# Memory's keys and values kept on chip: one pool of buffers in place of two, and stores issued by ScalarE

## The chip, the cores and the metric

The kernel runs on one core of one Trainium2 chip. The metric is the device time of one execution in microseconds (us). The engines are TensorE (PE; its weight loads are PEld), VectorE (DVE), ScalarE (ACT), GpSimd (POOL) and SyncE (SP), which here only issues transfers.

## The reference, cut to what matters

One layer of an encoder trunk over 1024 tokens of width 1024, in float32: latent attention and a Hyena operator side by side, then cross-attention into 256 memory tokens, then a mixture of experts. The change concerns only what the cross-attention takes from the memory tokens:

```python
def _mem_xattn(hx, hm, w_mq, w_mkv, w_mo):      # hm = _rms(mem, mem_norm_g): 256 x 1024
    q = (hx @ w_mq).reshape(B, S, MEM_HEADS, MEM_HEAD_DIM)        # 4 heads of 256
    k, v = jnp.split(hm @ w_mkv, 2, axis=-1)
    ...
    s = jnp.einsum('bshd,bmhd->bhsm', q, k).astype(jnp.float32) * MEM_HEAD_DIM ** -0.5
    p = jax.nn.softmax(s, axis=-1).astype(v.dtype)
    o = jnp.einsum('bhsm,bmhd->bshd', p, v).reshape(B, S, MEM_HEADS * MEM_HEAD_DIM)
    return o @ w_mo
```

Since `q k^T` is `hx (w_mq k^T)` and `(p v) w_mo` is `p (v w_mo)`, the kernel makes for each head the products of `w_mq` with the keys (KW) and of the values with `w_mo` (VW), both 1024 x 256 or 256 x 1024, once and ahead of time.

## The kernel before

**Split products.** Most matmuls work on pairs: `split` (line 196) rounds a float32 tile to a high part on ScalarE and subtracts it on VectorE for the low part; `mm3` (lines 204 to 208) adds three matmuls, high by high, high by low, low by high. A matmul of 256 or 512 columns in the profile is one of such three.

**Where memory's side stands.** `spectra` (line 287) is the first part of the program. It interleaves two streams of work that don't need each other: the filters of the Hyena operator (`filter_mlp`, `filters`: tiles `ph`, `win`, `eo`, `eoh`, `p`, `pp`, `q`, with tables `ftab` loaded by GpSimd's queue and results stored as `Kd` by SP's queue) and memory's side (`mem_side`, line 1198). Memory's side is a generator of 35 steps; `spectra` takes one or two of them after each step of the filters, until they are used up. When both are done, `x_rows` loads the tokens `xt` into the memory that they have left, and the projection follows. The order of tracing is the priority by which a planner fixes each engine's order of instructions at build time. On the chip each engine works through its own order, and a waiting instruction holds up those behind it.

**mem_side before.** First memory's rows are normalised and turned (`mx`, `mh` to `mmh`, `mml`). Then, in pools `mh` and `mhb`, 16 chunks of `w_mkv` (128 columns each, two for every head's keys, then two for every head's values): load `wm` (512 KB) by SP, split into `wmh`, `wml`, 24 matmuls of 256 columns into `pmk`, a copy by ScalarE to `mko`, and a store of 128 KB to `kvd` in HBM. Then these pools close and pool `mq` opens. For each of 4 heads of keys: `head` loads the head's two chunks back from `kvd` (`kv`, 256 KB) and splits them (`kvh`, `kvl`); `pair` splits two rows of `w_mq` (`qw` to `qwh`, `qwl`; `fetch` keeps two raw rows in flight); 48 matmuls make four `pkw` tiles; ScalarE scales them by `gc` into `mo` (line 1276, with high priority) and SP stores two 512 KB tiles of `mo` per head to KWd. For each of 4 heads of values the same with rows of `w_mo`: 24 matmuls of 512 columns (`pvw`), copies into `mo` (line 1292), two stores of 512 KB to VWd. KWd and VWd are read much later, by the cross-attention.

**PSUM.** The tiles `pmk`, `pkw` and `pvw` come from `psum1`, one bank each out of two buffers.

Of the kernel before, what the change touches and what calls it, by code (L numbers as in the profile page):

```python
# [9 lines left out]
F32 = mybir.dt.float32  # L10
F32R = mybir.dt.float32r
# [3 lines left out]
AF = mybir.ActivationFunctionType  # L15
ALU = mybir.AluOpType
# [6 lines left out]
P = 128  # L23
S = 1024
D = 1024
# [6 lines left out]
MEM = 256  # L32
MH, MHD = 4, 256
# [111 lines left out]
class Kern:  # L145
# [525 lines left out]
    def values(self):  # L671
        nc = self.nc
        self.ma = self.ma_cm.__enter__()
        self.V = self.ma.tile([P, NT, 512], F32, name="V")
        self.mla_rows(self.ma, self.key_rows(), 1)
        for i in range(NT):
            pv = self.psum1("pv")
            n, ts = i // 4, slice(i % 4 * P, i % 4 * P + P)
            (ch, cl), (wh, wl) = self.cqT[2], self.wm["v"]
            self.mm3(pv, ch[:, n, ts], cl[:, n, ts], wh, wl, True, True)  # L680
            nc.scalar.copy(self.V[:, i], pv)
            yield
# [515 lines left out]
    def mem_side(self):  # L1198

        nc, tc, a = self.nc, self.tc, self.a  # L1200
        kvd = self.dr.tile([16, P, MEM], F32, name="kvd")
        self.KWd = self.dr.tile([P, 8 * D], F32, name="KWd")
        self.VWd = self.dr.tile([P, 8 * D], F32, name="VWd")
        with tc.tile_pool(name="mh", bufs=1, side="right") as pa, tc.tile_pool(name="mhb", bufs=2, side="right") as pb:
            xts = [pb.tile([P, D], F32, tag="t4", name="mx", bufs=4) for i in range(2)]
            for i in range(2):
                nc.sync.dma_start(xts[i], a["mem"][i * P:(i + 1) * P])
            yield
            g = pb.tile([P, D], F32, tag="mw", name="mg")
            nc.sync.dma_start(g, a["mem_norm_g"].rearrange("(o n) -> o n", o=1).broadcast_to([P, D]))  # L1210
            mh = pa.tile([P, 8, MEM], F32R, name="mmh")
            ml = pa.tile([P, 8, MEM], F32R, name="mml")
            for i in range(2):
                h = self.rmsnorm(pb, xts[i], g, D, "m", 4)
                self.rows_T(pb, h, mh, ml, i)
                yield
            for c in range(16):
                w = pb.tile([P, 8, P], F32, tag="mw", name="wm")
                nc.sync.dma_start(w, a["w_mkv"][c])
                wh = pb.tile([P, 8, P], F32R, name="wmh")  # L1220
                wl = pb.tile([P, 8, P], F32R, name="wml")
                self.split(wh, wl, w)
                pk = self.psum1("pmk")[:, :MEM]
                for k in range(8):
                    self.mm3(pk, wh[:, k], wl[:, k], mh[:, k], ml[:, k], k == 0, k == 7)
                o = pb.tile([P, MEM], F32, name="mko")
                nc.scalar.copy(o, pk)
                nc.sync.dma_start(kvd[c], o)
                yield
        with tc.tile_pool(name="mq", bufs=2, side="right") as pb:  # L1230
            rows = [a["w_mqT"][j] for j in range(8)] + [a["w_mo"][j] for j in range(8)]
            raw = []

            def fetch():
                if rows:
                    w = pb.tile([P, D], F32, name="qw")
                    nc.sync.dma_start(w, rows.pop(0))
                    raw.append(w)

            fetch()  # L1240
            fetch()

            def pair():
                w = raw.pop(0)
                wh = pb.tile([P, D], F32R, name="qwh", bufs=3)
                wl = pb.tile([P, D], F32R, name="qwl", bufs=3)
                self.split(wh, wl, w)
                fetch()
                return wh, wl

            def head(j):
                t = pb.tile([P, 2, MEM], F32, name="kv", bufs=1)
                nc.sync.dma_start(t, kvd[j:j + 2].rearrange("c p m -> p c m"))
                th = pb.tile([P, 2, MEM], F32R, name="kvh")
                tl = pb.tile([P, 2, MEM], F32R, name="kvl")
                self.split(th, tl, t)
                return th, tl

            gc = pb.tile([P, 8], F32, name="gc", bufs=1)
            nc.sync.dma_start(gc, a["cross_norm_g"])  # L1260

            for h in range(MH):
                th, tl = head(2 * h)
                wp = [pair() for k in range(2)]
                for d0 in range(0, 8, 2):
                    pw = self.psum1("pkw")
                    if d0 % 4 == 0:
                        o = pb.tile([P, 4, MEM], F32, tag="mo", name="mo")
                    for d in range(2):
                        ds_ = slice((d0 + d) * P, (d0 + d + 1) * P)  # L1270
                        for k in range(2):
                            self.mm3(pw[:, d * MEM:(d + 1) * MEM], wp[k][0][:, ds_], wp[k][1][:, ds_], th[:, k], tl[:, k], k == 0, k == 1)
                    for d in range(2):
                        gd, src, j = gc[:, d0 + d:d0 + d + 1], pw[:, d * MEM:(d + 1) * MEM], d0 % 4 + d
                        with tc.high_priority():
                            nc.scalar.activation(o[:, j], src, AF.Identity, scale=gd)
                    if d0 % 4:
                        nc.sync.dma_start(self.KWd.rearrange("p (d m) -> p d m", d=8)[:, d0 - 2:d0 + 2, h * MEM:(h + 1) * MEM], o)
                        yield
            for h in range(MH):  # L1280
                th, tl = head(8 + 2 * h)
                wp = [pair() for k in range(2)]
                for mt in range(2):
                    ms = slice(mt * P, (mt + 1) * P)
                    o = pb.tile([P, 4, MEM], F32, tag="mo", name="mo")
                    for n in range(2):
                        pw = self.psum1("pvw")
                        ns = slice(n * 512, (n + 1) * 512)
                        for k in range(2):
                            self.mm3(pw, th[:, k, ms], tl[:, k, ms], wp[k][0][:, ns], wp[k][1][:, ns], k == 0, k == 1)  # L1290
                        with tc.high_priority():
                            nc.scalar.copy(o[:, 2 * n:2 * n + 2].rearrange("p a b -> p (a b)"), pw)
                    nc.sync.dma_start(self.VWd[:, (h * 2 + mt) * D:(h * 2 + mt + 1) * D], o.rearrange("p a b -> p (a b)"))
                    yield

    def cross_open(self):
        nc, tc, a = self.nc, self.tc, self.a
        self.h3d = self.dr.tile([S, D], F32, name="h3d")
        self.acc = self.dr.tile([S + NG * CAP, D], F32, name="acc")
        self.lg = self.late.tile([P, NT, 40], F32, name="lg")  # L1300
        self.route_init()
        wk = self.wk
        self.g3 = wk.tile([P, D], F32, tag="g", name="fg", bufs=1)
        nc.sync.dma_start(self.g3, a["ffn_norm_g"].rearrange("(o n) -> o n", o=1).broadcast_to([P, D]))
        self.wr = wk.tile([P, 8, 40], F32, name="wr")
        nc.sync.dma_start(self.wr, a["w_route"])
        gr = wk.tile([P, 8], F32, name="gr")
        nc.sync.dma_start(gr, a["ffn_gT"])
        nc.vector.tensor_tensor(self.wr, self.wr, gr[:, :, None].broadcast_to([P, 8, 40]), op=ALU.mult)
        self.br = self.bcast(wk, a["b_route"], 40, "br")  # L1310
        nc.vector.memset(self.br[:, 4:8], -3.0e38)
        self.hx, self.hT = {}, {}
# [790 lines left out]
```

## Time and profile before

| | before |
|---|---|
| time, median of 3 runs | 1499.66 us (1496.63 to 1503.1) |
| the profiled execution: its time / its span | 1501.6 / 1499.8 us |
| TensorE busy | 1373.0 us (92%), 6702 matmuls |
| VectorE / ScalarE / GpSimd busy | 1034.5 / 701.7 / 498.9 us |
| mean granted TensorE clock | 0.969 of full speed |

How to read the profile: it shows one execution, as seen by the hardware profiler. A row of the timeline has the start and duration in us, the engine (SPq is SP's queue of transfers), the line of the kernel, the operation, output <- inputs, shapes and count; in brackets, how long the engine idled before it and what ended that. A row of the lines view has a group's count, busy us and mean ns of one, then the idle time before it by what ended it. Matmuls overlap: the time from one start to the next is what one costs. The line of `mm3` (206 to 208) and `split` (196) are those of helpers, so tiles tell the stages apart.

### The profile page before, as it was taken

What the parts mean: (1) busy time and instruction counts of PE and PEld (TensorE: products, weight loads), DVE (VectorE), ACT (ScalarE), POOL (GpSimd) and SP (SyncE); (2) the same over time, 40 slices, a digit from 0 to 9 for tenths busy, and PEclk for the clock granted to TensorE, in tenths of its full rate; (3) what the DMA queues carried; (4) which work ended last, traced back from release to release, by engine and by line L of the source; (5) the groups of instructions that cost most, each with busy time, mean ns of one, the idle gap of its engine ahead of it and who ended that gap; (6) DMA issues with size and microseconds to landing.
All of it is one profiled execution on the core that took longest, in us unless ns stands there. A gap on an engine that the chain in (4) does not pass through costs nothing. (4 is left out here: it accounts for less than half of the span.)

```text
span 1499.8 us, 19038 instructions
## 1 busy us (share of the span) xinstructions
PE 1373.0 (92%) x6702; PEld 1025.5 (68%) x6702; DVE 1034.5 (69%) x1755; ACT 701.7 (47%) x1035; POOL 498.9 (33%) x363
## 2 busy tenths in 40 slices
PE   8888988999898989899899999999998999999990
PEld 5777767877787876565555788887886555666660
DVE  7655455389888888456657776434475598899985
ACT  6647446322212224434444344322232687888973
POOL 1321143354433242666666200000001238443322
PEclk9999999999999999999999999999999999999996
DMA  7458776343684525000311421004567899999995
GB/s 266 141 172 298 267 265 224 111 141 130 220 267 154 171 84 168 2 15 1 116 47 43 127 94 57 0 1 169 195 232 253 277 343 362 331 327 331 332 329 216
DMA packets 103406, 272.95 MB, mean 182 GB/s; under 512 B 13162, under 2 KB 41002, under 8 KB 103182
## 3 DMA queue, kind: packets, MB, share of 16 engines
q1 hardware_dynamic: 88590, 222.16, 42.3%
q0 software_dynamic: 14720, 49.57, 11.6%
q8 instruction: 53, 0.87, 0.2%
q14 instruction: 43, 0.35, 0.1%
HBM read 225.83 MB, written 50.07 MB: 184 GB/s over the span
## 5 line engine op out<-in xcount | busy, mean ns | idle before, releaser
L196 DVE TENSOR_TENSOR wt<-raw,wt 128x1024 fp32r<-128x1024 f32 x180 | 214.7, 1217 | 28.1 <-ACT wt L196 25.8
L196 ACT CAST wt<-raw 128x1024 fp32r<-128x1024 f32 x180 | 185.2, 1048 | 20.1 <-PE pgu L208 9.8
L994 POOL TENSOR_TENSOR sums<-sums,e 128x1024 f32<-128x1024 f32 x56 | 134.0, 2393 | 77.2 <-ACT e L990 75.4
L990 ACT ACTIVATE e<-psc 128x1024 f32<-128x1024 f32 x64 | 65.6, 1025 | 85.2 <-PE psc L208 81.9
L950 DVE TENSOR_REDUCE cn<-ptop 128x1 f32<-128x1024 f32 x64 | 75.7, 1211 | 41.2 <-PE ptop L949 40.8
L206 PE MATMUL pgu<-wt,xh 128*80 128x512 f32 x240 | 97.9, 408 | 0.0
L207 PE MATMUL pgu<-wt,xh 128*80 128x512 f32 x240 | 95.5, 398 | 0.0
L208 PE MATMUL pgu<-wt,xh 128*80 128x512 f32 x240 | 95.2, 397 | 0.0
L1835 POOL DMA_INDIRECT acc<-y,tab x28 | 51.2, 1827 | 118.9 <-ACT y L1832 100.7
L206 PE MATMUL psc<-xq,xk 97*128 97x512 f32 (+1 forms) x128 | 56.5, 441 | 11.3 <-ACT e L990 4.5
L1772 POOL DMA_INDIRECT xg<-h3d,tab x32 | 47.6, 1487 | 48.4 <-PE pxt L212 29.3
L999 PE MATMUL po<-e,V 128*64 128x512 f32 x256 | 58.5, 598 | 0.0
L362 POOL TENSOR_TENSOR eo<-win 128x512 f32<-128x512 f32 x16 | 23.8, 1488 | 87.8 <-DVE win L360 87.8
L206 PE MATMUL pw<-woh,ot 128*128 128x512 f32 x128 | 50.6, 395 | 1.6 <-DVE xr L1141 1.3
L207 PE MATMUL psc<-xq,xk 97*128 97x512 f32 (+1 forms) x128 | 52.0, 407 | 0.0
L208 PE MATMUL psc<-xq,xk 97*128 97x512 f32 (+1 forms) x128 | 52.0, 406 | 0.0
L233 POOL TENSOR_TENSOR fr<-fr0v,mhalf 128x1 f32<-128x1 f32 x4 | 2.3, 579 | 149.2 <-DVE fr0v L231 131.1
L572 ACT ACTIVATE uc<-pu,cw 128x1024 f32<-128x1024 f32 x12 | 14.5, 1209 | 78.6 <-PE pu L208 78.6
L206 PE MATMUL pcs<-kh,chh 128*128 128x512 f32 x128 | 50.4, 394 | 0.0
L207 PE MATMUL pw<-wol,ot 128*128 128x512 f32 x128 | 49.9, 390 | 0.0
L208 PE MATMUL pcs<-kh,chl 128*128 128x512 f32 x128 | 49.9, 389 | 0.0
L207 PE MATMUL pcs<-kl,chh 128*128 128x512 f32 x128 | 49.8, 389 | 0.0
(539 smaller groups left out, 4127.3 us busy)
## 6 DMA issues: line engine op xcount, KB each, us to landing
raw<-in_w_exp SPq DMA_DIRECT2D x192, 512.0 KB
tab<-in_t_cfwd POOLq DMA_DIRECT2D x32, 512.0 KB
ftab<-in_t_fwd POOLq DMA_DIRECT2D x16, 768.0 KB
wm<-in_w_mkv SPq DMA_DIRECT2D x16, 512.0 KB
Kd<-kts SPq DMA_DIRECT2D x16, 512.0 KB
kt<-Kd SPq DMA_DIRECT2D x32, 256.0 KB
tab<-in_t_inv SPq DMA_DIRECT2D x32, 256.0 KB
w<-in_w_hy SPq DMA_DIRECT2D x12, 512.0 KB
```

The source lines that it names most:

```text
L196: return self.nc.scalar.copy(hi, src).ins, self.nc.vector.tensor_tensor(lo, src, hi.bitcast(F32), op=ALU.subtract).ins
L206: mm(out, lh, rh, start=start, stop=False)
L207: mm(out, lh, rl, start=False, stop=False)
L208: mm(out, ll, rh, start=False, stop=stop)
L362: nc.gpsimd.tensor_tensor(t[:, 0], win[:, :512], win[:, 512:], op=ALU.add)
L572: nc.scalar.activation(y, pu, AF.Identity, scale=cw[:, c, 1:2], bias=cw[:, c, 3:4])
L950: nc.vector.tensor_reduce(cn[:, i, r:r + 1], ps, axis=AX.X, op=ALU.max, negate=True)
L990: nc.scalar.activation(e, ps, AF.Exp, scale=SCALE)
L994: nc.gpsimd.tensor_tensor(sums, sums, e, op=ALU.add)
L999: nc.tensor.matmul(po[par * 64:par * 64 + 64], V[:, kt, v], e[:, par * 512:(par + 1) * 512], start=kt == 0, stop=kt == NT - 1, skip_group_ ...
L1772: return nc.gpsimd.indirect_dma_start(out=x, out_offset=None, in_=self.h3d, in_offset=bass.IndirectOffsetOnAxis(ap=tok, axis=0), bounds_ch ...
L1835: scat = nc.gpsimd.indirect_dma_start(out=self.acc, out_offset=bass.IndirectOffsetOnAxis(ap=to, axis=0), in_=y, in_offset=None, bounds_che ...
```

## The change

`mem_side` keeps one pair of pools from beginning to end. Three kinds of 4 KB buffers (per partition), `mw` (raw, 2), `mwh` and `mwl` (3 each), hold memory's rows at first and then the raw, high and low weights of both kinds. The order of loads is a list: the two chunks of head 0, then for each of the 8 heads (4 of keys, 4 of values) its two chunks and the two rows of the head before. `values(h)` makes a head's two chunks and splits them straight from PSUM into `kvh`, `kvl`; `kvd` with its stores and loads is gone. The result of head h - 1 follows after the chunks of head h. Each `pkw` or `pvw` tile has its own `mo` buffer of 2 KB (two buffers, 4 KB before) and its own store of 256 KB, begun by ScalarE (`nc.scalar.dma_start`). `gc` is loaded at the beginning. The number of steps stays 35.

```diff
-            xts = [pb.tile([P, D], F32, tag="t4", name="mx", bufs=4) for i in range(2)]
+            W = lambda kind, name, dt=F32: pb.tile([P, D], dt, tag=kind, name=name, bufs=2 if kind == "mw" else 3)
+            xts = [W("mwh", "mx") for i in range(2)]
...
-            for c in range(16):
-                w = pb.tile([P, 8, P], F32, tag="mw", name="wm")
-                nc.sync.dma_start(w, a["w_mkv"][c])
-                wh = pb.tile([P, 8, P], F32R, name="wmh")
-                wl = pb.tile([P, 8, P], F32R, name="wml")
-                self.split(wh, wl, w)
-                pk = self.psum1("pmk")[:, :MEM]
-                for k in range(8):
-                    self.mm3(pk, wh[:, k], wl[:, k], mh[:, k], ml[:, k], k == 0, k == 7)
-                o = pb.tile([P, MEM], F32, name="mko")
-                nc.scalar.copy(o, pk)
-                nc.sync.dma_start(kvd[c], o)
-                yield
-        with tc.tile_pool(name="mq", bufs=2, side="right") as pb:
-            rows = [a["w_mqT"][j] for j in range(8)] + [a["w_mo"][j] for j in range(8)]
+            chunks = lambda h: [a["w_mkv"][2 * h + j].rearrange("p k c -> p (k c)") for j in range(2)]
+            rows = lambda h: [a["w_mqT" if h < MH else "w_mo"][2 * (h % MH) + j] for j in range(2)]
+            order = chunks(0)
+            for h in range(1, 2 * MH):
+                order += chunks(h) + rows(h - 1)
+            order += rows(2 * MH - 1)
             raw = []
...
             def pair():
                 w = raw.pop(0)
-                wh = pb.tile([P, D], F32R, name="qwh", bufs=3)
-                wl = pb.tile([P, D], F32R, name="qwl", bufs=3)
+                wh, wl = W("mwh", "mwhi", F32R), W("mwl", "mwlo", F32R)
                 self.split(wh, wl, w)
                 fetch()
                 return wh, wl
 
-            def head(j):
-                t = pb.tile([P, 2, MEM], F32, name="kv", bufs=1)
-                nc.sync.dma_start(t, kvd[j:j + 2].rearrange("c p m -> p c m"))
+            def values(h):
                 th = pb.tile([P, 2, MEM], F32R, name="kvh")
                 tl = pb.tile([P, 2, MEM], F32R, name="kvl")
-                self.split(th, tl, t)
-                return th, tl
+                for c in range(2):
+                    if len(raw) < 2:
+                        fetch()
+                    wh, wl = (t.rearrange("p (k c) -> p k c", k=8) for t in pair())
+                    pk = self.psum1("pmk")[:, :MEM]
+                    for k in range(8):
+                        self.mm3(pk, wh[:, k], wl[:, k], mh[:, k], ml[:, k], k == 0, k == 7)
+                    self.split(th[:, c], tl[:, c], pk)
+                    yield
+                kv[h] = th, tl
...
-                    if d0 % 4 == 0:
-                        o = pb.tile([P, 4, MEM], F32, tag="mo", name="mo")
+                    o = pb.tile([P, 2, MEM], F32, tag="mo", name="mo")
...
+                    nc.scalar.dma_start(self.KWd.rearrange("p (d m) -> p d m", d=8)[:, d0:d0 + 2, h * MEM:(h + 1) * MEM], o)
                     if d0 % 4:
-                        nc.sync.dma_start(self.KWd.rearrange("p (d m) -> p d m", d=8)[:, d0 - 2:d0 + 2, h * MEM:(h + 1) * MEM], o)
                         yield
...
                         with tc.high_priority():
-                            nc.scalar.copy(o[:, 2 * n:2 * n + 2].rearrange("p a b -> p (a b)"), pw)
-                    nc.sync.dma_start(self.VWd[:, (h * 2 + mt) * D:(h * 2 + mt + 1) * D], o.rearrange("p a b -> p (a b)"))
+                            nc.scalar.copy(o, pw)
+                        nc.scalar.dma_start(self.VWd[:, (h * 2 + mt) * D + n * 512:(h * 2 + mt) * D + (n + 1) * 512], o)
                     yield
+
+            kv = {}
+            mixed = lambda h: keys_mixed(h) if h < MH else values_mixed(h - MH)
+            yield from values(0)
+            for h in range(1, 2 * MH):
+                yield from values(h)
+                yield from mixed(h - 1)
+            yield from mixed(2 * MH - 1)
```

## Rows read from the trace of the kernel before

**Rows 1.** The page, part 1: busy us of each engine (share of the span).

```profile
PE 1373.0 (92%) x6702; PEld 1025.5 (68%) x6702; DVE 1034.5 (69%) x1755; ACT 701.7 (47%) x1035; POOL 498.9 (33%) x363
```

**Rows 2.** Stretches: length; PE, PEld, DVE, ACT, POOL busy; granted clock, DMA share, GB/s.

```profile
20.00:50.00 30.00, 27.95 (x195) 23.97 (x195) 25.33 (x35) 25.42 (x32) 0.00 (x0) 1.00 0.56 179
50.00:90.00 40.00, 36.04 (x239) 32.82 (x238) 22.91 (x18) 21.30 (x27) 16.82 (x11) 0.96 0.35 110
90.00:110.00 20.00, 14.86 (x78) 12.98 (x76) 12.99 (x9) 8.87 (x14) 6.10 (x6) 0.83 0.72 241
110.00:140.00 30.00, 24.73 (x172) 21.93 (x171) 19.23 (x19) 24.50 (x44) 6.20 (x5) 1.00 0.87 289
140.00:180.00 40.00, 38.42 (x165) 30.43 (x166) 18.28 (x17) 18.19 (x27) 4.96 (x6) 1.00 0.87 289
```

**Rows 3.** Timeline of TensorE, 92 to 108 us.

```profile
94.04 0.39 PE L208 MATMUL p<-eoh,ftab 128*128 128x512 f32 x1
94.27 0.39 PE L206 MATMUL p<-eoh,ftab 128*128 128x512 f32 x1
99.79 0.77 PE L206 MATMUL pkw<-kvh,qwh 128*128 128x256 f32 x2 [5.14 <-issue]
100.36 0.63 PE L207 MATMUL p<-eol,ftab 128*128 128x512 f32 x1
100.79 0.63 PE L208 MATMUL p<-eoh,ftab 128*128 128x512 f32 x1
...
106.27 0.28 PE L208 MATMUL pkw<-kvh,qwl 128*128 128x256 f32 x1
106.39 0.40 PE L206 MATMUL pp<-eoh,ftab 128*128 128x512 f32 x1
```

**Rows 4.** Timeline of the other engines, 86 to 100 us.

```profile
90.49 0.45 SPq L1253 DMA_DIRECT2D kv<-kvd  x1
...
95.09 1.04 ACT L196 CAST qwh<-qw 128x1024 fp32r<-128x1024 f32 x1 [6.51 <-DMA qw<-in_w_mqT]
...
99.08 0.62 ACT L196 CAST kvh<-kv 128x512 fp32r<-128x512 f32 x1 [1.50 <-DMA kv<-kvd]
```

**Rows 5.** Waits of SP's queue, 0 to 300 us: total, times, longest.

```profile
SPq L1228 <- ACT mko L1227: 38.9, 14, 6.6
...
SPq L470 <- PE ph L208: 16.7, 1, 16.7
```

**Rows 6.** Lines view of ScalarE, 20 to 180 us.

```profile
L196 ACT CAST qwh<-qw 128x1024 fp32r<-128x1024 f32 x16 | 16.9, 1054 | 11.7 <-DMA qw<-in_w_mqT 9.9 <-DMA qw<-in_w_mo 1.6
L196 ACT CAST wmh<-wm 128x1024 fp32r<-128x1024 f32 x15 | 15.6, 1048 | 5.9 <-DMA wm<-in_w_mkv 5.9
L1276 ACT ACTIVATE mo<-pkw,gc 128x256 f32<-128x256 f32 x32 | 13.4, 478 | 2.9 <-DMA KWd<-mo 1.9 <-PE pkw L208 1.0
...
L1292 ACT COPY mo<-pvw 128x512 f32<-128x512 f32 x16 | 9.1, 587 | 18.9 <-PE pvw L208 7.6 <-issue 5.7 <-DMA VWd<-mo 5.2
L1227 ACT COPY mko<-pmk 128x256 f32<-128x256 f32 x16 | 5.7, 364 | 4.8 <-PE pmk L208 3.8 <-issue 1.0
L196 ACT CAST kvh<-kv 128x512 fp32r<-128x512 f32 x8 | 5.0, 622 | 2.7 <-DMA kv<-kvd 2.7
```

**Rows 7.** Waits of TensorE, 20 to 180 us.

```profile
PE pmk L208 <- DVE wml L196: 5.2, 4, 3.1
...
PE pkw L206 <- ACT mo L1276: 2.5, 2, 1.7
```

**Rows 8.** Timelines of SP's queue and ScalarE around one store; the VWd stores (ns; first, last).

```profile
121.38 0.36 SPq L1278 DMA_DIRECT2D KWd<-mo  x1
...
127.60 0.84 ACT L1276 ACTIVATE mo<-pkw,gc 128x256 f32<-128x256 f32 x2 [1.90 <-DMA KWd<-mo]
...
L1293 SPq DMA_DIRECT2D VWd<-mo x8: 319/323/812, 144.2 to 180.3; - x8
```

More of the change, by code (lines that the diff above doesn't have):

```diff
@@ L1200, in mem_side @@
         nc, tc, a = self.nc, self.tc, self.a
-        kvd = self.dr.tile([16, P, MEM], F32, name="kvd")
         self.KWd = self.dr.tile([P, 8 * D], F32, name="KWd")
@@ L1208, in mem_side @@
             yield
-            g = pb.tile([P, D], F32, tag="mw", name="mg")
+            g = W("mw", "mg")
             nc.sync.dma_start(g, a["mem_norm_g"].rearrange("(o n) -> o n", o=1).broadcast_to([P, D]))
@@ L1212, in mem_side @@
             ml = pa.tile([P, 8, MEM], F32R, name="mml")
+            gc = pa.tile([P, 8], F32, name="gc")
+            nc.sync.dma_start(gc, a["cross_norm_g"])
             for i in range(2):
-                h = self.rmsnorm(pb, xts[i], g, D, "m", 4)
+                h, ss = W("mwl", "mh"), pa.tile([P, 1], F32, name=f"mss{i}")
+                nc.scalar.activation(h, xts[i], AF.Square, accum_out=ss)
+                r = self.rstd(pa, ss, D, f"mr{i}")
+                nc.vector.scalar_tensor_tensor(h, xts[i], r, g, op0=ALU.mult, op1=ALU.mult)
                 self.rows_T(pb, h, mh, ml, i)
                 yield
-            for c in range(16):
-                w = pb.tile([P, 8, P], F32, tag="mw", name="wm")
-                nc.sync.dma_start(w, a["w_mkv"][c])
-                wh = pb.tile([P, 8, P], F32R, name="wmh")
-                wl = pb.tile([P, 8, P], F32R, name="wml")
-                self.split(wh, wl, w)
-                pk = self.psum1("pmk")[:, :MEM]
-                for k in range(8):
-                    self.mm3(pk, wh[:, k], wl[:, k], mh[:, k], ml[:, k], k == 0, k == 7)
-                o = pb.tile([P, MEM], F32, name="mko")
-                nc.scalar.copy(o, pk)
-                nc.sync.dma_start(kvd[c], o)
-                yield
-        with tc.tile_pool(name="mq", bufs=2, side="right") as pb:
-            rows = [a["w_mqT"][j] for j in range(8)] + [a["w_mo"][j] for j in range(8)]
+            chunks = lambda h: [a["w_mkv"][2 * h + j].rearrange("p k c -> p (k c)") for j in range(2)]
[4 more added lines that the diff above has]
+            order += rows(2 * MH - 1)
             raw = []
             def fetch():
-                if rows:
-                    w = pb.tile([P, D], F32, name="qw")
-                    nc.sync.dma_start(w, rows.pop(0))
+                if order:
+                    w = W("mw", "mwr")
+                    nc.sync.dma_start(w, order.pop(0))
                     raw.append(w)
-            fetch()
             fetch()
@@ L1249, in pair, with keys_mixed @@
                 return wh, wl
-            def head(j):
-                t = pb.tile([P, 2, MEM], F32, name="kv", bufs=1)
-                nc.sync.dma_start(t, kvd[j:j + 2].rearrange("c p m -> p c m"))
+            def values(h):
                 th = pb.tile([P, 2, MEM], F32R, name="kvh")
                 tl = pb.tile([P, 2, MEM], F32R, name="kvl")
-                self.split(th, tl, t)
-                return th, tl
[L1259 to L1263, printed above, removed]
+                for c in range(2):
[8 more added lines that the diff above has]
+                kv[h] = th, tl
+            def keys_mixed(h):
+                th, tl = kv.pop(h)
                 wp = [pair() for k in range(2)]
@@ L1273, in mem_side, with values_mixed @@
                     for d in range(2):
-                        gd, src, j = gc[:, d0 + d:d0 + d + 1], pw[:, d * MEM:(d + 1) * MEM], d0 % 4 + d
+                        gd, src = gc[:, d0 + d:d0 + d + 1], pw[:, d * MEM:(d + 1) * MEM]
                         with tc.high_priority():
-                            nc.scalar.activation(o[:, j], src, AF.Identity, scale=gd)
+                            nc.scalar.activation(o[:, d], src, AF.Identity, scale=gd)
+                    nc.scalar.dma_start(self.KWd.rearrange("p (d m) -> p d m", d=8)[:, d0:d0 + 2, h * MEM:(h + 1) * MEM], o)
                     if d0 % 4:
-                        nc.sync.dma_start(self.KWd.rearrange("p (d m) -> p d m", d=8)[:, d0 - 2:d0 + 2, h * MEM:(h + 1) * MEM], o)
                         yield
-            for h in range(MH):
-                th, tl = head(8 + 2 * h)
+            def values_mixed(h):
+                th, tl = kv.pop(h + MH)
                 wp = [pair() for k in range(2)]
@@ L1284, in mem_side @@
                     ms = slice(mt * P, (mt + 1) * P)
-                    o = pb.tile([P, 4, MEM], F32, tag="mo", name="mo")
                     for n in range(2):
+                        o = pb.tile([P, 512], F32, tag="mo", name="mo")
                         pw = self.psum1("pvw")
```

## The prediction, made before the changed kernel was run

> **What bounds the kernel now.** The page's busy times come first [rows 1]. TensorE leads by far (92%); it works in order, so its holes are what can be won. Its busy time counts overlapped matmuls, so holes are looked for in stretches and in the timeline. The table of stretches [rows 2] covers the part in which memory's side (`mem_side`) runs beside the Hyena filters. It shows three things. 90 to 110 us is the worst stretch: TensorE busy 14.9 of 20 us at a mean granted clock of 0.83. ScalarE (ACT) is nearly full from 20 to 50 (25.4 of 30) and from 110 to 140 (24.5 of 30), and half idle between. The DMA engines stand at 0.87 from 110 to 180, at 0.35 from 50 to 90.
>
> The timeline of TensorE says what happens at 94 us [rows 3]. The `p` matmuls follow each other every 0.23 us; then the first `pkw` matmuls stand next in the queue, and nothing moves for 5.1 us. The work after it goes at half rate (0.43 us from start to start for 512 columns, the 1.2 GHz level after an idle engine) until about 105 us; at 106.2 the 256-column matmuls come every 0.12 us again. What the engine waited for is in the other timelines [rows 4]: the first keys are loaded back at 90.5, after the first pools have closed; ScalarE idles 6.5 us for the first rows of w_mq, loaded just before, then 1.5 us for the keys, whose cast begins at 99.1. It is the change of pools with the trip of the keys through memory that TensorE stands still for.
>
> A hole here moves everything behind it: the last gate of this part, the loads of x, waits on TensorE's own `ph` matmuls (the waits of SP's queue, 16.7 us) [rows 5], so all that follows begins earlier by what TensorE's order gains.
>
> **The change part by part.**
>
> *Pool change and kvd trip removed.* From the end of the last full-rate `p` (94.27 + 0.23 = 94.50) to the `pp` at 106.39 are 11.89 us. In them stand 5 `p` and 24 `pkw` matmuls: 5 x 0.23 + 24 x 0.12 = 4.0 us at full rate [rows 3]. So 7.9 us are lost, clock included. After the change keys_mixed(0) comes two chunks after its keys, in buffers that are already there: **-7.9 us**. From below: 5.1, if the clock drops elsewhere instead; from above 7.9.
>
> *Fewer and freer transfers.* 16 stores of 128 KB and 8 loads of 256 KB go (4 MB), and SP no longer holds loads behind stores: it waited 38.9 us in 14 places for `mko` before it could issue the next thing [rows 5]. What this can give is bounded by ScalarE's waits for transfers outside the hole [rows 6]: `wm` 5.9, `qw` 9.9 - 6.5 + 1.6 = 5.0, `kv` 2.7 - 1.5 = 1.2, and 5.2 for a VWd store, 17.3 in all. TensorE stood for splits of `wm` only 5.2 us [rows 7]. Between 0 and 5.2 I take **-2.5**: the loads themselves are as many and as big as before, with two raw buffers still, so about half of these waits should stay.
>
> The row says SP was not short of issue time, it waited. The Trainium skill (DMA: Bandwidth & Descriptors, section "Issuing engines are not separate DMA queues") goes further: a DMA begun on another engine runs on the same 16 engines, and only the sequencer's time for issuing is saved. By that rule the move of the stores alone is worth nothing and this term would be 0, the sum 1493.8; the trace agrees that the issue itself is short (0.36 us), but shows loads queued behind waiting stores, which the rule does not speak of.
>
> *ScalarE's work.* Gone: 16 `mko` copies x 0.364 = 5.8 us and 8 `kvh` casts x 0.622 = 5.0 us. New: 16 casts of 256 columns straight from PSUM, as `mko`'s row 0.364 = 5.8, and 32 store issues. No row has an issue on ScalarE; SP's takes 0.36 us [rows 8], so 32 x 0.36 = 11.5 us in which the activations behind it stand. Net +6.5 us in some 160 us. Activations (32 x 0.478) and copies (16 x 0.587) of the results stay [rows 6]. The first eight steps, which fall into 20 to 50 us, change most: eight chunks cost 8 x (1.048 + 0.364) = 11.3 us before; six chunks, two row splits, eight activations and four issues cost 8.5 + 2.1 + 3.8 + 1.4 = 15.8. With 25.4 of 30 us in use [rows 2] the added 4.5 us just fit, and from 110 us on ScalarE gets the lighter mix. Bounds 0 and +6.5; I take **+1.5**, a third of the 4.5, since in-order engines don't fill gaps fully. If that cover is gone, it is 4.5. VectorE subtracts the same elements as before, from PSUM, in 16 pieces for 8; its added fixed costs lie in its idle time (18.3 of 40 us busy at 140 to 180). But the PSUM buffer of a chunk is now freed by VectorE's subtraction, not by ScalarE's copy alone; with two such buffers shared by chunks and results, the second `pkw` of a head waits for it. Bounded by a `kvh` wait and by nothing, it is in the 1.5.
>
> *Half-size result buffers.* `mo` keeps two buffers, each now half as big, and a store per buffer. ScalarE's next activation into a buffer waits for its store to land, and every cast queued behind it on ScalarE waits too. The one store that can be timed was issued at 121.38 and let the activation go at 127.60: 6.2 us for 512 KB at a DMA share near 0.87 [rows 2, 8]. A store of 256 KB takes between half of that (3.1) and all of it. The side's 32 steps end with the last VWd store at 180.3 [rows 8]; taken from 17 us on, when memory's rows are turned, they are 5.1 us each, and the later ones make two results each: one per 2.5 us, so a buffer is wanted again 2 x 2.5 - 0.95 (two activations) = 4.1 us after it was filled. Each of the two later results of a head (16 in all) waits 0 to 2.1 us: 0 to 34 us of ScalarE. Of its waits for `mo` stores before (1.9 + 5.2 [rows 6]) TensorE saw up to half (2.5 for ACT `mo` [rows 7]), so 0 to +17. I take **+0.5**: the DMA engines carry 4 MB less and more evenly, which is nearer to 3.1 than to 6.2.
>
> TensorE's own work does not change (384 + 192 + 96 matmuls, the same shapes), nor does the number of steps that `spectra` takes from the side (35), nor the work per step: 24 matmuls of 256 columns (2.9 us) or 12 of 512 (2.8 us). Raw loads stay at two buffers. Nothing after 240 us is touched.
>
> Sum: -7.9 - 2.5 + 1.5 + 0.5 = **-8.4 us**. The profiled execution took 1501.6 (span 1499.8), 1.9 above the median 1499.66: it would come to 1493.2, and the median to **1491.3 us**. What this measurement can tell from no change is about 0.5%, 7.5 us (the three runs span 6.5), so the forecast lies just past it.
>
> **The rivals.**
>
> *More is won (0.20).* The evened load of ScalarE and of the DMA engines takes most of the other waits too: all 5.2 us for `wm` splits, and the 2.5 for ACT `mo` [rows 7]. For it: both loads are lopsided now [rows 2]. Against it: the waits for splits come from in-order queues as much as from late loads. -7.9 - 5.2 - 2.5 = -15.6, **1484**.
>
> *The hole goes, the gain is eaten (0.22).* Work that ScalarE gets between 20 and 50 us fully shows (+4.5), the loads' waits all stay, and in each of 8 heads the second result waits one cast of 0.364 for its PSUM buffer (+2.9): the hole is only spread. -7.9 + 7.4 = -0.5, **1499**. For it: ScalarE has 4.6 us left in that stretch. This is also the case in which the change doesn't do what it says, the weights' three shared buffers making chunk and result wait for each other.
>
> *Slower (0.18).* The two half buffers of `mo` wait for each store: at 6.2 us a store, 16 waits of 2.1 us, half of them seen by TensorE, are +17: -8.4 - 0.5 + 17 = +8.1, **1507.8**. It decides from a landing time of about 5.2 us on, where 16 waits of 1.1, half of them seen, are 8.8 us and eat the gain. For it: the one timed store. Against it: 256 KB, less traffic. The Trainium skill (Perfetto Trace Analysis, section "DMA Optimizations") speaks for this one: batching small transfers into larger ones raises throughput, and it names 2 KB to 4 KB; here VWd's rows go from 4 KB to 2 KB and the stores double in number. The trace before has no 2 KB store to set beside it.
>
> **How the numbers follow.** The forecast has 0.40, around 1491.3 (1487 to 1496), of which some 0.6 lie below 1492.2, the mark for faster by over 0.5%. Faster: 0.24 + 0.20, and a little of the third case, 0.46. Slower: 0.18. Same: 0.36. The range leaves out one tenth at each end: down into the second case, 1481, up to the last, 1507.
>
> **What would show it.** Right: no wait of 5 us before the first `pkw`; the granted clock at its full level there; the x loads 6 to 10 us earlier; matmul counts as before; ScalarE busier from 20 to 50. The second term: shorter waits for `wm`. The third: `pkw` or chunk matmuls waiting for casts before 50 us. The fourth: ScalarE's waits for KWd or VWd stores under about 3 us in all. Wrong: many such waits of 1 to 2 us, or TensorE's holes as long in sum as before but scattered; or a gain that is lost after 240 us, where I assume a plain shift.

## The result, and the profile after

The changed kernel takes 1512.88 us (median of 6 runs; one of them, 1937.32 us at a granted clock of 0.649, is left out of the ratio) against 1502.32 us for the kernel before on the same chip: ratio 1.0063, 95% interval 1.0040 to 1.0085. It is slower by 0.6%; faster by 0.6% was forecast. The profiled execution took 1512.82 us, its span is 1511.0.

Busy time of the engines (part 1 of the page, as [rows 1]) hardly moves:

```profile
PE 1378.7 (91%) x6702; PEld 1029.8 (68%) x6702; DVE 1032.0 (68%) x1763; ACT 695.2 (46%) x1025; POOL 500.2 (33%) x363
```

Same table of stretches as [rows 2], after:

```profile
20.00:50.00 30.00, 24.47 (x152) 19.84 (x151) 25.73 (x39) 20.65 (x29) 0.00 (x0) 0.89 0.57 176
50.00:90.00 40.00, 35.47 (x227) 30.35 (x226) 27.19 (x26) 28.09 (x39) 18.76 (x12) 1.00 0.46 150
90.00:110.00 20.00, 18.59 (x131) 16.43 (x129) 9.33 (x9) 11.49 (x18) 2.81 (x4) 1.00 0.78 240
110.00:140.00 30.00, 23.91 (x136) 21.76 (x136) 14.29 (x14) 14.49 (x22) 3.03 (x3) 0.89 0.58 197
140.00:180.00 40.00, 35.89 (x170) 29.60 (x168) 20.75 (x20) 15.40 (x21) 9.04 (x7) 0.96 0.65 222
```

The hole at 94 us is gone: 131 matmuls at full clock stand between 90 and 110, where there were 78 at 0.83. But 20 to 50 and 110 to 180, at full clock before, now run at 0.89 to 0.96 with a less busy TensorE. The first `pu` matmul, which follows this part, begins at 256.4 us; before it was 245.9. So the loss of about 10 us is made before it, and what follows (1254.6 us to the end of the span, 1253.9 before) is a plain shift.

What TensorE waits for, 20 to 200 us, after (against [rows 7]; `mwr`, `mwhi` and `mwlo` are the raw, high and low weights of both kinds):

```profile
PE pmk L206 <- ACT mo L1274: 6.2, 4, 3.6
PE pkw L208 <- DVE mwlo L196: 4.3, 3, 1.8
PE pvw L206 <- ACT mo L1291: 2.6, 1, 2.6
PE pmk L206 <- ACT mo L1291: 2.5, 1, 2.5
PE pkw L206 <- DVE kvl L196: 2.0, 1, 2.0
```

Waits for the eviction of a result (ACT `mo`) come to 11.3 us; before they were 2.5 for `pkw` and 1.2 for `pvw`. ScalarE's own waits in the same stretch say what holds these evictions up (against the `mo` rows of [rows 6]):

```profile
ACT mo L1291 <- DMA VWd<-mo: 12.2, 5, 4.9
ACT mo L1274 <- DMA KWd<-mo: 7.5, 2, 4.9
```

19.7 us for stores still under way, against 7.1 before. One of these waits in ScalarE's timeline, then in TensorE's the last matmul of the third result and the matmul that the wait holds back:

```profile
105.62 0.84 ACT L1274 ACTIVATE mo<-pkw,gc 128x256 f32<-128x256 f32 x2 [0.59 <-PE pkw L208]
106.49 0.37 ACTq L1275 DMA_DIRECT2D KWd<-mo  x1
106.96 0.84 ACT L1274 ACTIVATE mo<-pkw,gc 128x256 f32<-128x256 f32 x2 [0.50 <-ACT mo L1274]
107.83 0.37 ACTq L1275 DMA_DIRECT2D KWd<-mo  x1
112.74 0.84 ACT L1274 ACTIVATE mo<-pkw,gc 128x256 f32<-128x256 f32 x2 [4.94 <-DMA KWd<-mo]
```

```profile
107.92 0.28 PE L208 MATMUL pkw<-kvh,mwlo 128*128 128x256 f32 x1
...
113.63 0.39 PE L206 MATMUL pmk<-mmh,mwhi 128*128 128x256 f32 x1 [3.56 <-ACT mo L1274]
```

Two results are evicted 1.3 us apart and fill both buffers. The third is ready at 108.2, 1.7 us after the store of the first was begun (106.49), and waits for it until 112.74: that store took 6.25 us. Until then its PSUM bank is not free, and the next chunk (`pmk`) needs that bank. The view of the tile `mo` gives the issue of a store on ScalarE and the time to landing, in ns and us (min, median, max):

```profile
L1275 ACTq DMA_DIRECT2D KWd<-mo x16: 366/366/396, 42.5 to 115.3; - x16
L1292 ACTq DMA_DIRECT2D VWd<-mo x16: 326/326/343, 124.3 to 185.4; - x16
...
DMA to landing us min/median/max: 2.0/3.1/7.8
```

The waits of SP's queue, 20 to 240 us (against [rows 5]), are no longer for `mko`. Its loads now wait for the raw buffers that VectorE's subtractions free (91.9 us; before, `qwl` and `wml` together, 40.0), and the x loads behind them for TensorE's `ph`, as before:

```profile
SPq L1234 <- DVE mwlo L196: 91.9, 22, 9.1
SPq L407 <- DVE kts L406: 40.7, 9, 17.4
SPq L470 <- PE ph L208: 18.0, 1, 18.0
```

### The profile page after: what moved, and what is told of

It is laid out like the page before. It is cut to its first block, busy times and chain, and to the rows that moved or that the text cites. A ratio compares the mean times of both kernels' runs of the same rounds, so it can differ in the third digit from the quotient of the medians.

```text
span 1511.0 us, 18993 instructions
## 1 busy us (share of the span) xinstructions
PE 1378.7 (91%) x6702; PEld 1029.8 (68%) x6702; DVE 1032.0 (68%) x1763; ACT 695.2 (46%) x1025; POOL 500.2 (33%) x363
## 5 line engine op out<-in xcount | busy, mean ns | idle before, releaser
L196 DVE TENSOR_TENSOR mwlo<-mwr,mwhi 128x1024 fp32r<-128x1024 f32 x32 | 40.0, 1254 | 26.9 <-ACT mwhi L196 26.8
```

Source lines behind the costliest of these rows:

```text
L196: return self.nc.scalar.copy(hi, src).ins, self.nc.vector.tensor_tensor(lo, src, hi.bitcast(F32), op=ALU.subtract).ins
```

## The experiments

Each ratio is to the kernel before, measured on the same chip in the same session, with its 95% interval. "First pu" is where that matmul begins in the one profiled execution of a kernel; these executions lie up to 12 us from the median of their kernel, so small differences in it prove little.

**Result buffers (E1 to E6).** Theory: the two half-size `mo` buffers wait for their stores. Rivals: who begins the stores, or the weights' shared buffers and the order of the work.

E1, four half-size buffers in the changed kernel (shown for `pkw`, the same for `pvw`). Room for them comes from opening the pool of two small attention tiles later:

```
-                    o = pb.tile([P, 2, MEM], F32, tag="mo", name="mo")
+                    o = pb.tile([P, 2, MEM], F32, tag="mo", name="mo", bufs=4)
```

> The changed kernel with four result buffers (mo) of 2 KB in place of two; the 4 KB for it come from opening the pool of kr and cn (3 KB) after the filters instead of before. Theory A (the two half-size result buffers wait for their stores; ScalarE stands, and the PSUM bank behind it holds TensorE): ScalarE's waits for KWd and VWd stores fall from 19.7 us to under 3, TensorE's waits for mo (11.3 us) to under 3, and the time falls by 9 to 14 us against the changed kernel, to a ratio of 0.995 to 1.001 against the kernel before. Theory B (bursts of weight splits in the three shared buffers, and keys split out of PSUM by two engines, set the holes): the waits for stores go too, but others take their place, ratio 1.004 to 1.007.

1.0027 (1.0003 to 1.0052), first pu 250.1; ScalarE waits 2.2 us for stores, TensorE 1.7 for evictions. The waits go as theory A said, but the time falls by 5 us against the changed kernel and not by 9 to 14: it lies between the two forecasts. TensorE's waits for weight splits rise from 6.7 to 12.3 us.

E2, the result tiles of before (two of 4 KB, 16 stores of 512 KB) in the changed kernel, still begun by ScalarE:

```
-                    o = pb.tile([P, 2, MEM], F32, tag="mo", name="mo")
+                    if d0 % 4 == 0:
+                        o = pb.tile([P, 4, MEM], F32, tag="mo", name="mo")
...
-                        nc.scalar.dma_start(self.VWd[:, (h * 2 + mt) * D + n * 512:(h * 2 + mt) * D + (n + 1) * 512], o)
+                    nc.scalar.dma_start(self.VWd[:, (h * 2 + mt) * D:(h * 2 + mt + 1) * D], o.rearrange("p a b -> p (a b)"))
```

> The changed kernel with the result tiles and stores of the kernel before (two buffers of 4 KB, 16 stores of 512 KB), still begun by ScalarE, same 3 KB of room. Theory A, if the room in buffers is what counts: as with four buffers of 2 KB, ratio 0.995 to 1.002. If it is the number of stores in flight that counts, two stores of 512 KB still wait: ScalarE's waits for stores 4 to 10 us, ratio 1.000 to 1.005. Theory B: 1.004 to 1.007.

1.0005 (0.9987 to 1.0024); first pu 245.4. ScalarE's waits for stores and TensorE's for evictions:

```profile
ACT mo L1297 <- DMA VWd<-mo: 3.9, 1, 3.9
```

```profile
PE pvw L206 <- ACT mo L1297: 3.2, 1, 3.2
PE pmk L206 <- ACT mo L1280: 1.9, 1, 1.9
```

E3, the changed kernel with its 32 stores begun by SP (`nc.sync.dma_start` for `nc.scalar.dma_start`):

> The changed kernel with its 32 stores begun by SP instead of ScalarE, nothing else. Theory A: SP's queue also holds the loads, which wait for raw buffers (92.6 us in 23 places), so a store goes out later, the result buffers come free later, and the time grows by 5 to 20 us over the changed kernel, ratio 1.010 to 1.020. Theory C (the issue on ScalarE is the cost: 32 x 0.35 = 11 us of ScalarE): the time falls by 4 to 10 us, ratio 0.999 to 1.004.

1.0106 (1.0087 to 1.0126), first pu 260.8. In SP's queue the stores wait for the evictions, and the loads stand behind them; ScalarE's waits for weights to arrive rise from 7.6 to 19.4 us:

```profile
SPq L1275 <- ACT mo L1274: 32.6, 16, 4.6
SPq L1292 <- ACT mo L1291: 28.0, 12, 6.4
```

E4, the kernel before with nothing but the half-size result buffers, stored in 256 KB pieces begun by ScalarE:

> The kernel before with one part of the change alone: each pkw or pvw tile has its own 2 KB result buffer (two of them), stored by ScalarE as 256 KB. Theory A: slower by 5 to 15 us, ratio 1.003 to 1.010, with 10 us or more of ScalarE waiting for KWd and VWd stores. Theory B: no change beyond 3 us, ratio 0.998 to 1.002.

1.0093 (1.0071 to 1.0116), first pu 265.7. Its ScalarE waits 19.0 us for stores, its TensorE 14.2 for evictions, with the hole still there (`issue`):

```profile
ACT mo L1275 <- DMA KWd<-mo: 10.9, 6, 3.1
ACT mo L1291 <- DMA VWd<-mo: 4.1, 4, 1.5
ACT mo L1291 <- DMA KWd<-mo: 4.0, 1, 4.0
```

```profile
PE pvw L206 <- ACT mo L1291: 8.3, 4, 3.1
PE pkw L206 <- issue: 5.9, 1, 5.9
PE pkw L206 <- ACT mo L1275: 5.2, 7, 1.5
```

E5, control: the changed kernel with the later pool alone (`kr` and `cn` from a pool opened after the spectra):

> The changed kernel with only the two small tiles of the attention part (kr, cn) moved into a pool that opens later, which is how the four-buffer and the big-buffer kernels found their room; result buffers stay two of 2 KB. If the result buffers alone explain what those kernels won back, this one stands where the changed kernel does: 1.004 to 1.009 of the kernel before, ScalarE waiting 15 to 20 us for KWd and VWd stores before 200 us. If the later pool itself helped, it comes to 1.000 to 1.003, and the credit given to the buffers was wrong.

1.0054 (1.0029 to 1.0078), 18.1 us of waits for stores: the pool explains nothing.

E6, the kernel before with its 512 KB stores begun by ScalarE:

> The kernel before with its 16 result stores of 512 KB begun by ScalarE in place of SP, nothing else. If the loss of the half-size result buffers alone (1.0093) comes from their size, this one stays within 0.3% of the kernel before, with 4 to 8 us of ScalarE's waits for stores as before. If it comes from ScalarE issuing the stores, it goes to about half of that loss or more (half as many issues of 0.35 us): 1.004 to 1.009.

0.9971 (0.9953 to 0.9990): not a loss but a gain of 4 us, the lowest ratio of all kernels here that leave nothing out. ScalarE's waits for stores (7.5 us before) are gone, and TensorE's for evictions fall from 3.7 to 0.8; ScalarE's waits for loads do not fall (20.1 before, 22.9). So it is the result buffers that come free sooner, and not the loads that arrive sooner. Its first pu (247.6) is no earlier in the profile, so where the 4 us are won is not shown.

Half-size buffers in the kernel before thus cost 1.0093 (E4) against 0.9971, some 18 us, and as much by the first pu (265.7 against 247.6). In the changed kernel they cost 1.0063 against 1.0005 (E2), some 9 us (256.4 against 245.4 by the first pu). The theory holds for the size of the buffers; four half-size ones (E1) win back about 5 us only.

**Where the hole's gain went (E7 to E17).** E2 has no hole and few waits for stores (3.9 us), and yet only equals the kernel before. TensorE's waits between 20 and 200 us add up to 17.7 us in it; before, they are 18.5, of which 5.1 are the hole. The stretch in which the first results are made shows a part of this. Two windows of it, columns as in [rows 2]; first the kernel before, then the changed kernel, then E2:

```profile
28.00:36.00 8.00, 7.15 (x58) 6.74 (x57) 7.63 (x13) 7.94 (x11) 0.00 (x0) 1.00 0.52 182
36.00:44.00 8.00, 6.80 (x46) 5.44 (x46) 7.71 (x10) 7.16 (x9) 0.00 (x0) 1.00 0.47 146
```

```profile
28.00:36.00 8.00, 5.53 (x36) 4.12 (x34) 5.83 (x10) 5.61 (x9) 0.00 (x0) 1.00 0.49 147
36.00:44.00 8.00, 6.04 (x23) 4.17 (x22) 6.47 (x12) 5.42 (x10) 0.00 (x0) 0.57 0.28 81
```

```profile
28.00:36.00 8.00, 6.24 (x40) 4.68 (x39) 7.28 (x13) 6.43 (x10) 0.00 (x0) 1.00 0.45 143
36.00:44.00 8.00, 6.66 (x37) 5.50 (x36) 7.11 (x11) 5.99 (x11) 0.00 (x0) 0.79 0.39 132
```

In the changed kernel TensorE waits there for two of VectorE's results:

```profile
35.53 0.39 PE L206 MATMUL pkw<-kvh,mwhi 128*128 128x256 f32 x1 [1.99 <-DVE kvl L196]
39.11 0.58 PE L208 MATMUL pkw<-kvh,mwlo 128*128 128x256 f32 x1 [1.82 <-DVE mwlo L196]
```

But VectorE is less busy in these 16 us than before (12.30 us for 15.33). It stands for a cast of ScalarE, which stands for its load:

```profile
29.84 1.05 ACT L196 CAST mwhi<-mwr 128x1024 fp32r<-128x1024 f32 x1 [1.49 <-DMA mwr<-in_w_mqT]
30.92 1.23 DVE L196 TENSOR_TENSOR mwlo<-mwr,mwhi 128x1024 fp32r<-128x1024 f32 x1 [1.79 <-ACT mwhi L196]
```

And a load waits for a raw buffer, which VectorE's subtraction frees, so that each of the three waits for another.

E7, E2 with weights split up to two tiles ahead of their use:

```
+            def ahead(n):
+                while len(made) < n and raw:
...
                     self.split(th[:, c], tl[:, c], pk)
+                    ahead(2)
                     yield
```

> The changed kernel with the big result buffers (two of 4 KB, 512 KB stores) and the weights split up to two tiles ahead of their use: the rows of w_mq and w_mo are split in the steps of the chunks before them, the next chunk during the results. Same buffers, same loads in the same order. If the gain of the removed hole was eaten by splits that begin only when their result step does (waits of TensorE for mwlo and mwhi, 8 to 10 us between 15 and 200 us), these waits fall to under 4 us and the time to 0.995 to 0.998 of the kernel before. If these waits only show another limit (ScalarE and VectorE in order, the two raw buffers, loads), the waits move to other tiles and the time stays at 0.999 to 1.002, as with the big buffers alone.

0.9985 (0.9957 to 1.0012), first pu 247.0: not to be told from E2. TensorE still waits 6.8 us for weight splits (8.5 in E2) and 2.9 for `kvl` (1.6). E8, besides, the chunks' splits at the planner's high priority:

> As the kernel with weights split ahead, and besides the split of a chunk's keys or values out of PSUM (kvh, kvl) is given the planner's high priority, as the result evictions have. In the changed kernel the first pkw stands 2.0 us for kvl at 33 us. If that wait is from VectorE's order, it goes, and the time falls by up to 2 us against the kernel without it (0.995 to 0.997 of before). If the planner then puts other work later, there is no difference or a small loss.

1.0006 (0.9982 to 1.0030): no gain; TensorE still waited 1.7 us for `kvl` at 33.7 us. E9, E7 with GpSimd in VectorE's place for four weight tiles:

```
+                    if k in (4, 5, 8, 9):
+                        nc.scalar.copy(wh, w)
+                        nc.gpsimd.tensor_tensor(wl, w, wh.bitcast(F32), op=ALU.subtract)
```

> The kernel with big result buffers and weights split ahead, in which GpSimd (idle from 20 to 50 us) makes the low halves of the w_mq rows of the first two heads, four subtractions of 128x1024, in VectorE's place. In all kernels with keys on chip TensorE stands 3 to 4 us at the first pkw (33 to 40 us) for kvl and mwlo, both VectorE's, and then goes at half clock from 36 to 44 us; the kernel before does neither. If VectorE's queue in that stretch is what eats the gain of the removed hole, the mwlo waits there go, the clock stays up, and the time falls by 3 to 6 us against the kernel without it (to 0.994 to 0.997 of before). If the first result step is late for another reason (loads, ScalarE, the longer chain of casts), the low clock from 36 to 44 us stays and so does the time (0.998 to 1.001).

1.0039 (1.0014 to 1.0065): worse than either forecast, though its first pu (246.4) is no later than E7's; the clock is 0.50 from 36 to 44. The timelines of GpSimd and VectorE show why this did not relieve VectorE:

```profile
30.87 2.37 POOL L1254 TENSOR_TENSOR mwlo<-mwr,mwhi 128x1024 fp32r<-128x1024 f32 x1 [20.00 <-ACT mwhi L1253]
38.63 2.84 POOL L1254 TENSOR_TENSOR mwlo<-mwr,mwhi 128x1024 fp32r<-128x1024 f32 x1 [5.39 <-ACT mwhi L1253]
```

```profile
29.78 0.68 DVE L279 SCALAR_TENSOR_TENSOR u<-k,u 64x512 f32<-64x512 f32 x1
31.43 2.35 DVE L279 SCALAR_TENSOR_TENSOR u<-k,u 64x512 f32<-64x512 f32 x1
37.85 4.17 DVE L279 SCALAR_TENSOR_TENSOR u<-k,u 64x512 f32<-64x512 f32 x3
```

E10, the first result one head later (`bufs=3` for `kvh` and `kvl`, half-size result buffers), and E11, its control with two:

> The changed kernel with weights split ahead (half-size result buffers), and three buffers for a head's keys or values in place of two, so that six chunks stand ahead of the first result and the first pkw comes two chunks later, after the filter's first stage. If the first result step collides with the filter's start on VectorE, the waits at 33 to 40 us and the low clock after them go or get shorter, and the time is 3 to 6 us under the control with two buffers. If the waits only move with it, it equals the control within 2 us.

> Control for the later first result: the changed kernel with weights split ahead and the later pool for two small tiles, half-size result buffers. If waiting for stores is what the changed kernel loses by, splitting ahead does not help it: 1.003 to 1.007 of before, ScalarE still waiting 15 to 20 us for stores. If the splits were the cause, it is at 0.998 to 1.001.

E10: 1.0085 (1.0053 to 1.0116); E11: 1.0064 (1.0036 to 1.0092), with 14.3 us of waits for stores. Later is no better. The wait moved with the result (3.3 us for `kvl` at 45 us). E12, E6 with four low halves of chunks on GpSimd:

> The kernel before with its 512 KB stores begun by ScalarE, and the low halves of chunks 3 to 6 of w_mkv made by GpSimd in VectorE's place. TensorE waited 2.8 us for these (wml) between 29 and 43 us. If VectorE's queue is what TensorE waits for there, these waits go and the time falls by 2 to 3 us more (0.994 to 0.997 of before); if GpSimd's subtraction, slower than VectorE's 1.2 us, comes later than VectorE's would, the time is the same or 1 to 3 us longer.

1.0046 (1.0020 to 1.0072): 11 us worse than E6, more than forecast; TensorE waits for GpSimd instead, up to 2.0 us a tile. E13, shared buffers and no change of pools, but all chunks first and keys through memory:

```
+            order = sum([chunks(h) for h in range(2 * MH)], []) + sum([rows(h) for h in range(2 * MH)], [])
...
+                tl = kv.pop(h)
+                th = pb.tile([P, 2, MEM], F32R, name="kvh")
+                self.split(th, tl, tl.bitcast(F32))
+                load(h + 1)
```

> Half of the change: weights of both kinds share buffers and are split ahead, results are stored in 512 KB pieces begun by ScalarE, but all 16 chunks come first and keys and values still go through memory (eight 256 KB stores, eight loads one head ahead). So there is no change of pools and no hole at the first pkw, and no early results between the chunks. If the hole was worth its 7.9 us, and it is the early results among the chunks that cost it again, this kernel beats the kernel before with stores by ScalarE (0.9971): 0.991 to 0.994 of before. If removing the hole is worth little wherever it is done, because TensorE then stands for something else, it is at 0.996 to 0.999.

1.0013 (0.9987 to 1.0038), first pu 248.0: neither theory. The hole at 94 us is gone here too, but another of the same size opened at 68 us, where the chunk's weight cast stands behind an `eoh` cast that waits for GpSimd:

```profile
73.50 0.58 PE L206 MATMUL pmk<-mmh,mwhi 128*128 128x256 f32 x1 [5.54 <-ACT mwhi L196]
```

```profile
71.18 1.05 ACT L196 CAST eoh<-eo 128x1024 fp32r<-128x1024 f32 x1 [4.81 <-POOL eo L363]
72.40 1.99 ACT L196 CAST mwhi<-mwr 128x1024 fp32r<-128x1024 f32 x2
```

E14, E7 without VectorE's early low halves (`wl = wh` for 14 weight tiles, `tl = th` for three heads), and E15, the same for ten chunks of E6:

> The kernel with big buffers and weights split ahead, with part of the work left out: for the first 14 weight tiles and the first three heads' keys the low half is not made (VectorE's subtraction), and TensorE uses the high half in its place, with the same matmuls. It stands against the same omission in the kernel before (next run). If VectorE's subtractions are why the first 50 us got worse with the keys on chip, the waits at 33 to 40 us and the half clock after them go, and this one gains 4 to 6 us against the kernel with them (to 0.994 to 0.996), more than the kernel before gains by it. If ScalarE's casts or the loads are what is late there, it gains 2 us or less.

> The kernel before with 512 KB stores by ScalarE, with part of the work left out: for the first ten chunks the low half of the weights is not made, and TensorE uses the high half in its place. TensorE waited 2.8 us for these subtractions before 50 us and 3.1 us at 66 us. If it follows VectorE there, the time falls by 2 to 5 us against the kernel with them (to 0.994 to 0.996 of before); if other waits take their place, it stays at 0.996 to 0.998.

E14: 0.9927 (0.9901 to 0.9953), 0.6% under E7; first pu 238.3, 8.7 us earlier. E15: first pu 247.28 for E6's 247.64. Its whole time (1.0211) can't be compared: the experts' matmuls (`pgu`) begin when they did in E6, at 1157.6, but it makes 48 of them from raw weights where all other kernels make 32, the last at 1515.0 (E6's last begins at 1457.0). That other values send more tokens to some expert is argued, not shown. Up to `pu`, then, leaving these subtractions out gives the on-chip kernel 8.4 us more than the kernel before.

E16 leaves out the keys' low halves alone, E17 the weight tiles' alone:

> The kernel with big buffers and weights split ahead, with one part of the work left out: the low half of the first three heads' keys (VectorE's subtraction of 128x256 from PSUM, six of them), TensorE using the high half in its place; so ScalarE's cast alone frees the PSUM bank of these chunks, which the next result takes. The kernel without these and without the low halves of the first 14 weight tiles began its first pu 8.7 us earlier than the kernel with all. If the PSUM bank held for VectorE is the reason, this run shows most of it: no half clock from 36 to 44 us and the first pu 5 to 8 us earlier than 247. If it is the weight tiles, the first pu stays at 245 to 248.

> The other half: the low halves of the first 14 weight tiles are left out (VectorE's subtraction of 128x1024, 1.2 us each), those of the keys are made. If VectorE's time for the weight tiles is the reason, the first pu comes 5 to 8 us earlier than 247 and the half clock from 36 to 44 us is gone. If the PSUM bank of the chunks is the reason, the wait for kvl at 33 us stays, and the first pu is at 244 to 248.

E16: 0.9985 (0.9961 to 1.0009), first pu 244.8; E17: 0.9986 (0.9960 to 1.0012), first pu 239.9, 7.1 us earlier than E7. The two windows, E16 and E17:

```profile
28.00:36.00 8.00, 6.07 (x40) 4.67 (x38) 4.64 (x8) 4.58 (x8) 0.00 (x0) 0.93 0.60 156
36.00:44.00 8.00, 4.97 (x14) 3.07 (x15) 7.83 (x13) 6.03 (x7) 0.00 (x0) 0.50 0.10 24
```

```profile
28.00:36.00 8.00, 7.14 (x49) 5.99 (x50) 7.68 (x15) 6.15 (x9) 0.00 (x0) 1.00 0.71 217
36.00:44.00 8.00, 7.07 (x51) 5.92 (x50) 5.43 (x10) 6.91 (x13) 0.00 (x0) 1.00 0.62 206
```

With the weight tiles' subtractions gone, 100 matmuls stand in these 16 us at full clock; with the keys' gone, 54. So in the profiles the first results come in time without the low halves of the weight tiles. How these hold them up is not shown: their subtraction is waited for by TensorE, and it also frees the raw buffer for the next load. E17 does away with both, and no run has a third raw buffer. Nor is E16 a clean counterpart: 4.2 us of its second window are a wait of the filters' `ph` for ScalarE, which E7 does not have.

By whole times this is only half settled. E14 keeps its gain to the end; E17 does not: its profiled execution is 5.4 us shorter than E7's, its ratio equal. What a kernel's executions differ by seems to lie behind `pu`: E5 and the changed kernel begin it at 255.9 and 256.4, though E5's profiled execution was 6.3 us under its median. There TensorE's waits at the convolution's `pf` (for `z`, or for nothing that shows) run from 7.6 to 20.1 us, and not by how early a kernel gets there: 20.1 in E14 (238.3) and 18.1 in E2 (245.4), but 19.6 in E3 (260.8) and 16.1 in E11 (258.5). All four of these executions were slower than the median of their kernel. Where E17's 7 us went stays open.

## Why the prediction was wrong

*Half-size result buffers (+0.5): the step that failed.* It measured about +9 in this kernel and +18 alone. The rate of results was mis-sized: one per 2.5 us was worked out from the mean length of a step, so that a buffer had 4.1 us. In the timeline the results of a head come in one burst: the third is ready 1.7 us after the store that it waits for was begun. The landing time taken was not wrong in the median (3.1 us, the lower bound used), but the waits come from the slow ones (up to 7.8); the 6.2 us of the one timed store of [rows 8] came back (6.25), though for half the bytes. And TensorE saw 11.3 of 19.7 us, about the half that the bound had. The rival "Slower" had this mechanism and gave 1507.8, but with 16 waits of 2.1 us; they were 7, of up to 4.9.

*Pool change and kvd trip (-7.9).* The hole went as predicted, with its clock. But E2, which takes the buffers' price away, leaves 0.5 us of the 7.9 by the first pu, and none by the time. Part of it came back in the first eight steps, by waits for `kvl` and `mwlo` and then half clock: between 28 and 44 us there were 104 matmuls before, 59 in the changed kernel and 77 in E2, which is 45 x 0.12 = 5.4 us and 27 x 0.12 = 3.2 us (estimates, at the pace of 256 columns). The rest of E2's loss is in no one place that was found. The step that failed here is that what fills the hole would be ready in time.

*ScalarE's work (+1.5).* Right stretch, wrong reason. ScalarE was less busy from 20 to 50 (20.65 us for 25.42), not more. E14 and E17 put the wait on the weights' low halves, which VectorE makes and whose cost had been called idle-time work by a later stretch (140 to 180 us). It is not that VectorE is full; by its place in the chain of load, cast, subtraction and freed buffer it is late. The wait of a result for the PSUM bank that `kvl` frees, named there, is not the main thing: no wait for `kvl` in the changed kernel is longer than 2.0 us, and E16, without `kvl` in the first three heads, begins `pu` 2.3 us earlier than E7, E17 7.1.

*Fewer and freer transfers (-2.5).* Not found. TensorE's waits for weight splits were 8.9 us in all (the 5.2 of [rows 7] among them); they are 8.5 in E2, and 6.7 in the changed kernel, which lost more than that at the evictions. What does help is keeping stores out of the loads' queue: E6 gains 0.3%, with no waits for stores left, though its loads arrive no sooner; E3 loses 0.4% against the changed kernel, its loads standing behind stores. The prediction set the Trainium skill (DMA: Bandwidth & Descriptors, section "Issuing engines are not separate DMA queues") against the row of SP's waits; the runs side with the row. That the issue itself is short agrees, 0.33 to 0.37 us against 3.1 us to landing; what costs in E3 is the load queued behind a store that waits.

*Outside 20 to 240 us*, a plain shift: right for the changed kernel (1254.6 us from first pu to the end, 1253.9 before), not for every profiled execution of the experiments (1247 to 1264, E15 aside).

"The hole goes, the gain is eaten" (-0.5) describes E2, though by other waits than it named; with the buffers' price of 9 us it makes +8.5, and the ratio of 1.0063 is +9.5.

## What to carry to other kernels

Halving a buffer while keeping two of them halves the time that a store has, and what counts is the gap between two results inside a burst, read from the timeline, not the mean pace. Stores begun by the engine that made the data cost little (E6), and keep waiting stores out of the queue that brings the loads (E3). A hole in an in-order engine is worth its length only if what fills it is ready there: look at the place from which the filling work is taken, and at the chain of loads and splits that feeds it.

## What the runs showed of the hardware

A GpSimd subtraction of 128x1024 took 2.37 to 2.84 us, and VectorE's operation beside it 2.35 us for 0.68 (E9). The Trainium skill (SBUF — State Buffer, section "SBUF: two separate sides") says that the two share a port pair as an exclusive lock: a GpSimd operation that reads SBUF and a VectorE operation with two inputs in SBUF, as these are, block one another for a whole instruction. The trace agrees: VectorE's operation, begun at 31.43 us while GpSimd worked until 33.24, ended at 33.78. Idle GpSimd is no free help to VectorE here.

In the changed kernel two waits of about 2 us, for `kvl` and `mwlo` near 34 and 38 us, came with a stretch at 1.2 GHz: granted 0.57 from 36 to 44 us, where the kernel before had 1.00. By an estimate at most 8 x 0.43 = 3.4 us are lost by the clock, since the second wait (1.8 us) falls into it; the two waits are 3.8 us.
